# A decoder block's query weights asked for earlier, its expert numbers put first, its head squares summed on another engine

## The chip, the cores and the metric

The kernel runs on one core of one Trainium2 chip. A core has a matrix engine (TensorE, PE in the profile, with its weight loads as PEld), a vector engine (VectorE, DVE), a scalar engine (ScalarE, ACT), a general engine (GpSimd, POOL), a queue engine that issues most transfers (SyncE, SP) and 16 DMA engines that carry them out. Every engine works through its own instructions in order and waits for semaphores of the others. The metric is the device time of one execution in microseconds (us).

## What is computed

One decoder layer over 512 tokens of width 1024, in float32. Three attention branches (a forgetting attention, a windowed one and one over 256 memory tokens) are mixed with sigmoid gates, projected and added to x. Then each token looks up experts: its query, 8 heads of 2 x 128, is scored against 2 x 128 keys, the best 16 of each half are paired, the best 16 pairs of each head name 128 of the 16384 experts, and

```
experts = e1 * N_KEYS + e2
gates = softmax(sv)
a[e] = dot(h, u[experts[e]])
out = sum_e gelu(a[e]) * gates[e] * v[experts[e]]
```

Queries and keys of the attention branches are normalised by head first: each head's 64 (or 128) values are squared and summed, and the head is scaled by one over the root of the mean.

## The kernel before

The 512 tokens are four blocks of 128. Block 0 goes through the mixers alone (`mixers(0, ...)`), and then blocks 1 to 3 go through them together (`mixers(1, ...)`, `BIG` = 3 blocks). While the three are mixed, block 0's expert search and its expert rows run beside them: `beside()` is a generator, and `pump()`, called at every load of weights and by every head of the attentions, lets it go on by some steps. After the mixers the three blocks are searched, and then all experts are computed densely for blocks 2 and 3 (the long stage from about 720 us on), while blocks 0 and 1 go on gathering single expert rows.

The order in which each engine gets its instructions up to the dense stage is laid out ahead of time by a planner. It simulates the kernel on a timeline of its own, with priorities that follow the program's order. What `pump()` issues after the search is put 400 steps later in priority, so that it fills gaps. A dependency that only fixes an order (`add_manual_dep` with `NoSync`) keeps one instruction behind another in that planning. From the dense stage on the order of PE, DVE and POOL is the one written.

Block 0's search (`search` with one block) takes 16 tiles of query weights of 512 KB each, two per head. `fetch` asks for a tile on SP's queue when its product is issued. The tiles turn over in four slots: three lie in the buffer that will hold the three blocks' merged branches (`mg1`), one (`raw`) in memory that the first mixers' weights occupied. PE multiplies (line 766), ACT copies the query out (767), PE scores it against the keys (774), ACT copies the scores (777), and DVE picks the best 16 of each half and of the pairs (lines 731 to 735).

After that, in `beside()`: `weigh` makes the softmax of the found values (lines 801 to 813, on DVE with one exponential on ACT), and `numbers_of` turns the found positions into expert numbers (`choose`, lines 828 to 858, then 868 and 869) and makes block 0's normalised row `own` (line 872). Then `step` asks POOL for each expert's row (line 908), and DVE multiplies it with `own` and sums (line 929) or adds it into the output (lines 936, 939, 942). 184 such rows are issued beside the mixers.

In the mixers, `heads` computes one group of queries or keys: products (lines 152 to 154, three for each pair of split operands), then in `use`, for each block, a copy out of PSUM on ACT (348), the square of the product on ACT (350) and the sum by head on DVE (351). `rsqrt_mean` (209 and 210) makes the factors, and ACT scales each head by its factor (363). Buffers for queries (`qT`) and for the branch output (`ohi`, `olo`) have one slot each.

Of the kernel before, what the change touches and what calls it, by code (L numbers as in the profile page):

```python
# [8 lines left out]
F32 = mybir.dt.float32  # L9
# [4 lines left out]
AF = mybir.ActivationFunctionType  # L14
OP = mybir.AluOpType
AX = mybir.AxisListType

S, D, NB, KC = 512, 1024, 4, 8
NMEM = 256
EPS = 1e-6  # L20
TOPK = 16
# [38 lines left out]
def tile_block(ctx: ExitStack, tc: tile.TileContext, t: dict, out: bass.AP):  # L60
# [98 lines left out]
    def wide(tag, nb, dt=F32):  # L159

        slot = big.tile([128, (1 if tag == "mg0" else BIG) * D], dt, tag=tag, name=tag)
        return slot[:, :nb * D]

    def by_token(x):
        return x.rearrange("p (b d) -> p b d", d=D)
# [175 lines left out]
    def heads(lhs, src, nb, nh, hd, pad=0, n=None, also=None, fetch=None, cast=None):  # L341

        z = pp.tile([128, BIG, 4 * 66], F32, tag="qn", name="qn")
        z = z[:, :nb, :nh * (hd + pad)].rearrange("p b (h d) -> p b h d", h=nh)
        ss = small_f(BIG * 4, "hss")[:, :nb * nh]

        def use(b, ps):
            A.copy(z[:, b, :, :hd], ps[:, :nh * hd].rearrange("p (h d) -> p h d", h=nh))
            sq = pp.tile([128, 256], F32, tag="sq", name="sq")[:, :nh * hd]
            A.square(sq, ps[:, :nh * hd])  # L350
            V.reduce_sum(ss[:, b * nh:b * nh + nh], sq.rearrange("p (h d) -> p h d", h=nh), axis=AX.X)
            if also:
                also(b, ps)

        gemm_nat(lhs, src, n or nh * hd, nb, use, fetch=fetch, cast=cast)
        r = rsqrt_mean(ss, nb * nh, hd)
        for b in range(nb):
            if nb < BIG:
                V.tensor_mul(z[:, b, :, :hd], z[:, b, :, :hd],
                             r[:, b * nh:b * nh + nh, None].to_broadcast([128, nh, hd]))  # L360
                continue
            for h in range(nh):
                A.activation(z[:, b, h, :hd], z[:, b, h, :hd], AF.Copy, scale=r[:, b * nh + h:b * nh + h + 1])
        return z
# [429 lines left out]
        yield from top_pairs(PH - 1)  # L794


    def weigh(pool, f, g):

        nb = len(GROUPS[g])
        ex = pool.tile([128, nb, PH, TOPK], F32, name="ex")  # L800
        V.tensor_sub(ex, f.best, f.best[:, :, :, 0:1].to_broadcast([128, nb, PH, TOPK]))
        for b in range(nb):
            bf = ex[:, b].rearrange("p h s -> p (h s)")
            ins = A.activation(bf, bf, AF.Exp, scale=rstd[:, GROUPS[g][b]:GROUPS[g][b] + 1])
            if b:
                tc.keep_in_program_order(ins)
        yield 0.4
        den = small.tile([128, BIG * PH], F32, tag="gden", name="gden", bufs=1)[:, :nb * PH]
        dv = den.rearrange("p (b h) -> p b h", b=nb)
        V.reduce_sum(dv, ex, axis=AX.X)  # L810
        V.reciprocal(den, den)
        for b in range(nb):
            V.tensor_mul(gates_of[g][:, b].rearrange("p s h -> p h s"), ex[:, b],
                         dv[:, b, :, None].to_broadcast([128, PH, TOPK]))
        yield 1.0
# [42 lines left out]
            V.tensor_add(dst[i], hv[:, 0], hv[:, 1])  # L858
            yield 1.4

    def numbers_of(pool, f, lb, b, iota_k):

        g2r = pool.tile([128, D], F32, name="g2r")
        row = t["g2_row"]
        nc.sync.dma_start(g2r, bass.AP(tensor=row.tensor, offset=row.offset, ap=[[0, 128], [1, D]]))
        e = [pool.tile([128, NJ], F32, tag=f"e{i}", name=f"e{i}") for i in range(2)]
        yield from choose(pool, f, lb, iota_k, e)
        V.scalar_tensor_tensor(e[0], e[0], float(NK), e[1], op0=OP.mult, op1=OP.add)
        V.tensor_copy(eidx[b], e[0])
        if b == 0:  # L870
            h2n[0] = h2n[1] = ep.tile([128, D], F32, tag="own", name="own")
        V.scalar_tensor_tensor(h2n[b], x1[b], rstd[:, b:b + 1], g2r, op0=OP.mult, op1=OP.mult)
        yield 1.3


# [74 lines left out]
    def beside():  # L950
# [3 lines left out]
        with tc.tile_pool(name="qa", bufs=2, side="right") as qq:  # L954
            h2T = chunks(qq.tile([128, KC, 128], F32, name="aT", bufs=1))
            behind.append(turn([x1[0]], g2, h2T, None).ins.name)
            V.tensor_copy(rstd[:, 0:1], factors(sums, 1))
            yield 0.0
            lent, turns = by_token(wide("mg1", BIG)), [0]

            def fetch(src, n):
                i = turns[0] % (BIG + 1)
                turns[0] += 1
                raw = lent[:, i] if i < BIG else qq.tile([128, D], F32, tag="raw", name="raw", bufs=1)
                fill(raw, src, n)
                return raw

            yield from search(qq, h2T, f, 1, fetch)
        pace[0] = "choose"
        share[0] = 0.0  # L970
        with tc.tile_pool(name="ca", bufs=1, side="right") as pool:
            iota_k = iota_of(pool)
            yield from weigh(pool, f, 0)
            yield from numbers_of(pool, f, 0, 0, iota_k)
        kept.close()
        pace[0], share[0] = "rows", 0.0
        credit[0] += 20.0
# [445 lines left out]
```

## Time and profile before

| | |
|---|---|
| three runs | 1552.81, 1552.13 and 1544.93 us, median 1552.13 |
| profiled execution | 1548.8 us, its span from first to last instruction 1547.0 us |
| mean granted TensorE clock | 0.99 |
| PE, DVE, ACT, POOL busy | 97%, 92%, 53% and 50% of the span |
| DMA | 533.48 MB, mean 345 GB/s |

The profile is one execution, recorded by the hardware. A row of a timeline gives the start and the duration in us, the engine, the line of the kernel, the operation, what it writes and reads, its shape, and in brackets how long the engine had been idle before it and what released it. A row of waits gives who waited for whom, then the total in us, the number of times and the longest. Busy time of PE is no measure of its efficiency, since products overlap.

### The profile page before, as it was taken

The numbers are of one execution on the slowest core, as the hardware profiler recorded it, in microseconds if no ns is written. First come the engines' busy times: TensorE is split into PE (matmuls) and PEld (weight loads), VectorE is DVE, ScalarE is ACT, GpSimd is POOL, SyncE is SP. The second block draws the span as 40 slices with busy tenths as digits, with TensorE's granted clock in tenths as the row PEclk, the third lists the DMA queues.
The fourth block names the chain that finished last, engine by engine and source line by source line (L and its number), as shares of the span: only waits on it lengthen the run. The fifth ranks groups of instructions, "written<-read, shape, count | busy, mean of one in ns | idle before, by whom it ended". The sixth has DMA issues, their size and how long they took to land.

```text
span 1547.0 us, 27092 instructions
## 1 busy us (share of the span) xinstructions
PE 1498.3 (97%) x9411; PEld 1360.5 (88%) x9411; DVE 1419.4 (92%) x2673; ACT 812.4 (53%) x1806; POOL 778.1 (50%) x642
## 2 busy tenths in 40 slices
PE   8999999999999989999999999999999999999998
PEld 7999899997897989999888887788888888888887
DVE  6689488989999999999999999899999999999998
ACT  7778346646345533352225899545444544544543
POOL 1101016767667456877445666545554544555451
PEclk9999999999998999999999999999999999999999
DMA  8688657998999898986998999999999999999995
GB/s 325 207 289 300 246 174 280 338 362 302 360 367 325 293 356 317 352 310 232 327 365 329 393 395 384 373 397 398 401 410 403 408 410 404 411 410 410 410 410 209
DMA packets 180125, 533.48 MB, mean 345 GB/s; under 512 B 17660, under 2 KB 48148, under 8 KB 179988
## 3 DMA queue, kind: packets, MB, share of 16 engines
q0 software_dynamic: 73728, 268.47, 45.9%
q1 hardware_dynamic: 96180, 227.54, 40.1%
q10 hardware_dynamic: 10080, 35.75, 5.8%
q8 instruction: 74, 1.21, 0.3%
q14 instruction: 63, 0.52, 0.1%
HBM read 516.99 MB, written 14.69 MB: 344 GB/s over the span
## 4 chain that ended last, share of the span: by engine, by line
PE 52%; issue 14%; DMA 11%; POOL 9%; DVE 9%; ACT 4%; POOLq 0%; DVEq 0%; SPq 0%; ACTq 0%
PE mm L153 9%; PE mm L152 9%; PE mm L154 9%; POOL row L908 9%; PE mm L1078 5%; DMA row<-in_peer_v_dram,eidx 4%; DMA row<-in_peer_u_dram,eidx 3%; PE sc L1078 3%; DVE wlo L138 2%; DMA gd<-st 2%; PE mm L766 2%; DVE o L1144 2%; DVE scr L929 1%; PE tp L384 1%; PE sc L506 1%
## 5 line engine op out<-in xcount | busy, mean ns | idle before, releaser
L908 POOL DMA_INDIRECT row<-in_peer_v_dram,eidx x256 | 322.2, 1258 | 298.3 <-DVE two L942 175.5
L908 POOL DMA_INDIRECT row<-in_peer_u_dram,eidx x256 | 315.4, 1232 | 219.8 <-DVE scr L929 115.8
L138 DVE TENSOR_TENSOR wlo<-raw,whi 128x1024 fp32r<-128x1024 f32 (+1 forms) x228 | 277.2, 1220 | 21.7 <-ACT whi L123 17.5
L942 DVE SCALAR_TENSOR_TENSOR two<-row,acts,two 128x1024 f32<-128x1024 f32 x197 | 252.6, 1282 | 5.3 <-DMA row<-in_peer_v_dram,eidx 3.1
L123 ACT CAST whi<-raw 128x1024 fp32r<-128x1024 f32 x146 | 152.2, 1050 | 119.2 <-PE mm L153 75.4
L929 DVE SCALAR_TENSOR_TENSOR scr<-row,own 128x1024 bf16<-128x1024 f32 x128 | 156.2, 1220 | 7.1 <-DMA row<-in_peer_u_dram,eidx 6.4
L929 DVE SCALAR_TENSOR_TENSOR scr<-row,two 128x1024 bf16<-128x1024 f32 x115 | 139.5, 1213 | 3.8 <-DMA row<-in_peer_u_dram,eidx 2.9
L210 POOL TENSOR_TENSOR rsy<-rsv,mhalf 128x4 f32<-128x4 f32 (+5 forms) x25 | 37.8, 1515 | 177.2 <-DVE rsv L209 176.3
L1212 ACT CAST ah<-ga 128x256 fp32r<-128x256 f32 x116 | 47.1, 407 | 150.2 <-PE tp L153 125.0
L152 PE MATMUL mm<-hhi,whi 128*128 128x384 f32 x320 | 110.8, 346 | 1.8 <-ACT hhi L244 1.4
L153 PE MATMUL mm<-hlo,whi 128*128 128x384 f32 x320 | 110.7, 346 | 0.0
L154 PE MATMUL mm<-hhi,wlo 128*128 128x384 f32 x320 | 109.9, 343 | 0.0
L152 PE MATMUL mm<-whi,hhi 128*128 128x256 f32 (+1 forms) x360 | 103.6, 290 | 2.7 <-ACT hhi L681 1.9
L1214 ACT CAST whi<-raw 128x1024 fp32r<-128x1024 f32 x96 | 100.3, 1047 | 9.5 <-DMA raw<-in_peer_v_dram 4.6
L153 PE MATMUL mm<-wlo,hhi 128*128 128x256 f32 (+1 forms) x360 | 102.7, 286 | 1.3 <-DVE wlo L138 1.3
L153 PE MATMUL sc<-wlo,ah 128*128 128x512 f32 x256 | 101.2, 395 | 2.5 <-DVE wlo L138 2.5
L152 PE MATMUL sc<-whi,ah 128*128 128x512 f32 x256 | 100.8, 394 | 1.3 <-ACT whi L1214 1.2
L154 PE MATMUL mm<-whi,hlo 128*128 128x256 f32 (+1 forms) x360 | 102.0, 285 | 0.0
L154 PE MATMUL sc<-whi,al 128*128 128x512 f32 x256 | 101.2, 395 | 0.0
L153 PE MATMUL tp<-wlo,ah 128*128 128x512 f32 x256 | 101.1, 395 | 0.0
L152 PE MATMUL tp<-whi,ah 128*128 128x512 f32 x256 | 101.0, 395 | 0.0
L154 PE MATMUL tp<-whi,al 128*128 128x512 f32 x256 | 100.6, 393 | 0.0
(332 smaller groups left out, 4478.2 us busy)
## 6 DMA issues: line engine op xcount, KB each, us to landing
raw<-in_peer_v_dram SPq DMA_DIRECT2D x96, 512.0 KB
hhi<-in_uT_dram ACTq DMA_DIRECT2D x68, 512.0 KB
raw<-in_w_tr_dram SPq DMA_DIRECT2D x48, 512.0 KB
raw<-in_w_nat_dram SPq DMA_DIRECT2D x40, 512.0 KB
last<-in_peer_v_dram SPq DMA_DIRECT2D x32, 512.0 KB
hhi<-in_uT_dram SPq DMA_DIRECT2D x26, 512.0 KB
raw<-in_w_o_dram SPq DMA_DIRECT2D x24, 512.0 KB
gd<-st SPq DMA_DIRECT2D x24, 512.0 KB
```

The source lines that it names most:

```text
L123: ins = (cast or A.copy)(hi[:, :n * w], raw[:, :n * w])
L138: V.tensor_sub(lo, raw, hi.bitcast(F32))
L152: PE.matmul(ps, lh, rh, start=first, stop=False)
L153: PE.matmul(ps, lh, rl, start=False, stop=False)
L154: PE.matmul(ps, ll, rh, start=False, stop=last)
L210: G.tensor_tensor(y, v, mhalf[:, :n], op=OP.pow)
L908: ins = G.indirect_dma_start(out=r, out_offset=None, in_=t["peer_" + tab], in_offset=bass.IndirectOffsetOnAxis(ap=eidx[b][:, j:j + 1], axi ...
L929: V.scalar_tensor_tensor(scr, r, 1.0, two[0] if b else h2n[b], op0=OP.mult, op1=OP.mult, accum_out=acts[b][:, c]))
L942: V.scalar_tensor_tensor(two[0], r, acts[b][:, c], two[0], op0=OP.mult, op1=OP.add))
L1078: PE.matmul(ps[:, :TD], w[:, dc], h2f[dc], start=dc == 0, stop=dc == KC - 1)
L1212: A.copy(ah, a)
L1214: A.copy(hi, raw)
```

## The change

It has three parts.

1. `fetch` has seven slots in place of four: the same three of `mg1`, the one called `raw`, and one each in the buffers `qT`, `ohi` and `olo`. At the first product it asks for seven tiles, and at each later one for the next tile, up to 16.
2. `numbers_of` goes before `weigh`. An order-only dependency (`follow`) puts the weighing's first instruction and the row `own` behind the copy of the expert numbers.
3. In `heads`, where three blocks are worked on together, ACT squares each head by itself out of the copy `z` and sums it with the same instruction (`accum_out`). The square of the whole group and DVE's sum by head are left out there. Block 0 and the memory tokens keep the earlier way.

```diff
@@ heads / use
-            A.square(sq, ps[:, :nh * hd])
-            V.reduce_sum(ss[:, b * nh:b * nh + nh], sq.rearrange("p (h d) -> p h d", h=nh), axis=AX.X)
+            if nb == BIG:
+                for h in range(nh):
+                    A.activation(sq[:, h * hd:(h + 1) * hd], z[:, b, h, :hd], AF.Square,
+                                 accum_out=ss[:, b * nh + h:b * nh + h + 1])
+            else:
+                A.square(sq, ps[:, :nh * hd])
+                V.reduce_sum(ss[:, b * nh:b * nh + nh], sq.rearrange("p (h d) -> p h d", h=nh), axis=AX.X)
@@ weigh
+    def follow(ins, after):
+        if after:
+            tc.add_manual_dep(ins.ins, after[-1], mybir.DependencyInfo(
+                mybir.DependencyClass.NoSync, mybir.DependencyReason.DATA), reason="behind the numbers")
+
-    def weigh(pool, f, g):
+    def weigh(pool, f, g, after=()):
...
-        V.tensor_sub(ex, f.best, f.best[:, :, :, 0:1].to_broadcast([128, nb, PH, TOPK]))
+        follow(V.tensor_sub(ex, f.best, f.best[:, :, :, 0:1].to_broadcast([128, nb, PH, TOPK])), after)
@@ numbers_of
-    def numbers_of(pool, f, lb, b, iota_k):
+    def numbers_of(pool, f, lb, b, iota_k, done=None):
...
-        V.tensor_copy(eidx[b], e[0])
+        ins = V.tensor_copy(eidx[b], e[0])
+        if done is not None:
+            done.append(ins.ins.name)
...
-        V.scalar_tensor_tensor(h2n[b], x1[b], rstd[:, b:b + 1], g2r, op0=OP.mult, op1=OP.mult)
+        follow(V.scalar_tensor_tensor(h2n[b], x1[b], rstd[:, b:b + 1], g2r, op0=OP.mult, op1=OP.mult), done)
@@ beside
-            lent, turns = by_token(wide("mg1", BIG)), [0]
+            lent = by_token(wide("mg1", BIG))
+            slots = [lent[:, i] for i in range(BIG)] + [qq.tile([128, D], F32, tag="raw", name="raw", bufs=1)]
+            slots += [pp.tile([128, 4, BIG * 128], F32, tag=tag, name="raw", bufs=1).rearrange("p a b -> p (a b)")[:, :D]
+                      for tag in ("qT", "ohi", "olo")]
+            asked, taken = [0], [0]
 
             def fetch(src, n):
-                i = turns[0] % (BIG + 1)
-                turns[0] += 1
-                raw = lent[:, i] if i < BIG else qq.tile([128, D], F32, tag="raw", name="raw", bufs=1)
-                fill(raw, src, n)
-                return raw
+                i = taken[0]
+                taken[0] += 1
+                while asked[0] < min(i + len(slots), 2 * PH):
+                    fill(slots[asked[0] % len(slots)], t["w_pq"][asked[0]], n)
+                    asked[0] += 1
+                return slots[i % len(slots)]
...
-            yield from weigh(pool, f, 0)
-            yield from numbers_of(pool, f, 0, 0, iota_k)
+            numbered = []
+            yield from numbers_of(pool, f, 0, 0, iota_k, numbered)
+            yield from weigh(pool, f, 0, numbered)
```

## The prediction

> **What bounds the kernel now.** I read the page's totals first, then the busy time by stages, then the waits and the order of time in the stages that the change touches.
>
> ```profile
> span 1547.0 us, 27092 instructions
> PE 1498.3 (97%) x9411; PEld 1360.5 (88%) x9411; DVE 1419.4 (92%) x2673; ACT 812.4 (53%) x1806; POOL 778.1 (50%) x642
> ```
>
> TensorE is idle for only 1547.0 - 1498.3 = 48.7 us, and VectorE for 128. ScalarE is free half of the time. By stages (columns: stretch, its length, busy us of PE, PEld, DVE, ACT, POOL, clock, DMA share, GB/s):
>
> ```profile
> 177.00:212.40 35.40, 32.83 (x291) 32.28 (x289) 24.07 (x150) 10.90 (x32) 5.40 (x25) 1.00 0.79 276
> 212.40:244.00 31.60, 31.60 (x271) 31.60 (x270) 29.68 (x112) 20.21 (x60) 7.42 (x11) 1.00 0.31 102
> 244.00:480.00 236.00, 231.68 (x1603) 211.80 (x1602) 214.73 (x404) 128.75 (x326) 168.45 (x126) 1.00 0.95 346
> 480.00:500.00 20.00, 16.36 (x75) 13.90 (x75) 18.98 (x37) 9.57 (x24) 16.29 (x12) 0.74 0.95 333
> 560.00:630.00 70.00, 62.45 (x426) 59.85 (x425) 68.59 (x82) 26.39 (x52) 41.02 (x29) 0.93 0.90 317
> 630.00:720.00 90.00, 88.97 (x541) 87.13 (x540) 87.15 (x492) 36.95 (x63) 70.98 (x70) 1.00 0.82 304
> 1000.00:1500.00 500.00, 496.63 (x2908) 437.58 (x2907) 489.13 (x570) 243.96 (x355) 252.85 (x186) 1.00 1.02 406
> ```
>
> Block 0's search lies in the first stretch, its expert numbers in the second, the three blocks' mixers with the gathered rows from 244 to about 630, their search after that. From 1000 to 1500 PE lacks 3.4 us of 500: what is left there is work, so that a shift before it should pass through to the end. What can be won before 630 is PE's idle time, 2.6 + 0 + 4.3 + 3.6 + 7.6 = 18.1 us in the five stretches shown, and time at a lowered clock: (1 - 0.74) x 20 + (1 - 0.93) x 70 = 10.1 us. In 560 to 630 DVE is full (68.59 of 70) and PE waits for it:
>
> ```profile
> PE mm L152 <- DVE g L618: 2.2, 2, 1.4
> PE mm L152 <- ACT hhi L681: 1.9, 1, 1.9
> ```
>
> Both are products of DVE or come right behind them, and the gathered rows, 1.2 us each, are what else is in DVE's queue.
>
> The lowered clock follows waits of PE. The wait that opens the stretch at 480 is this one:
>
> ```profile
> 482.67 0.44 PE L384 MATMUL tp<-cst,p 128*128 128x128 f32 x2 [2.12 <-ACT p L547]
> ```
>
> [...]
>
> **Part 1, seven weight tiles.** Four slots of 512 KB turn over in block 0's search. PE stops for them:
>
> ```profile
> 188.71 3.84 PE L766 MATMUL mm<-aT,mg 128*128 128x128 f32 x32 [1.31 <-DMA mg<-in_w_pq_dram]
> ...
> 193.62 2.05 PE L766 MATMUL mm<-aT,raw 128*128 128x128 f32 x16 [1.07 <-DMA raw<-in_w_pq_dram]
> ```
>
> ```profile
> 157.52 0.80 SPq L117 DMA_DIRECT2D mg<-in_w_pq_dram  x2
> ...
> 184.84 0.33 SPq L117 DMA_DIRECT2D raw<-in_w_pq_dram  x1
> ```
>
> The tile asked for at 184.84 is the one that PE takes at 193.62: 8.8 us. A tile with its share of scores costs PE 32.83 / 16 = 2.05 us. Four slots give 4 x 2.05 = 8.2 us of lead, less than 8.8; seven give 14.4. So these waits, 1.31 + 1.07 = 2.4 us of the stretch's 2.6 idle, go. The first seven asks are now ahead of the search: three more transfers, 1.5 MB, on SP's queue, near the ones that already go out at 157.52, 20 us before the search. At the 276 GB/s of the first stretch they take 5.7 us, inside that time. If they stood behind the fourth tile, whose buffer comes free only shortly before the search, they would still land within 14 us, and tile 4 isn't read before 177 + 4 x 2.05 = 185.2. Bounds of this part: 0 (they come late or push the mixers' weights back) to -2.4; I take -2.4, as 14.4 is far over 8.8. The borrowed buffers (query, and the two halves of the branch output) are next written by the mixers' own code after 244, when the search is over: no new wait.
>
> **Part 2, numbers first.** Between search and rows DVE does this (first and last of the weighing's four instructions, the normalised block, the numbers, the first row):
>
> ```profile
> 220.70 0.29 DVE L801 TENSOR_TENSOR ex<-best 128x128 f32<-128x128 f32 x1
> ...
> 225.50 0.41 DVE L813 TENSOR_TENSOR gate<-ex,gden 128x128 f32<-128x128 f32 x1
> ...
> 225.82 1.28 DVE L872 SCALAR_TENSOR_TENSOR own<-mg,rstd,g2r 128x1024 f32<-128x1024 f32 x1
> ...
> 241.11 0.23 DVE L869 CAST eidx<-e 128x128 int32<-128x128 f32 x1
> ...
> 249.53 1.23 DVE L929 SCALAR_TENSOR_TENSOR scr<-row,own 128x1024 bf16<-128x1024 f32 x1 [5.06 <-DMA row<-in_peer_u_dram,eidx]
> ```
>
> ```profile
> 242.34 1.58 POOL L908 DMA_INDIRECT row<-in_peer_u_dram,eidx  x1 [5.18 <-ACT sq L350]
> ```
>
> Moved behind the numbers: the weighing, 4 x about 0.25 = 1.0 us, and the block's 1.2 us (1.28 less overlap). Neither is late there. The block is read by the first row at 249.53, 7.2 us after POOL asks for it; the weighing's result is wanted only when all 128 rows of u are through. With part 1's 2.4 us and some five reductions, about 1.5 us, gone from this stretch (part 3), the numbers come 2.4 + 1.0 + 1.2 + 1.5 = 6.1 us sooner, near 235, and the first gather near 236. POOL sits idle before 242.34, so nothing is pushed back by it but the small powers on the same queue, by at most one gather, 1.58 us. If all of this is only slack, its worth is 0; if DVE bounds without a break until 720, it is 6.1.
>
> **Part 3, squares on ScalarE.** Removed from DVE and from ACT in the three blocks (210 to 490; durations are minimum, median and maximum in ns):
>
> ```profile
> L351 DVE TENSOR_REDUCE hss<-sq x27: 270/412/421, 216.1 to 480.4; 128x4 f32<-128x256 f32 x18, 128x2 f32<-128x256 f32 x6, 128x2 f32<-128x128 f32 x3
> ```
>
> ```profile
> L350 ACT ACTIVATE sq<-mm x27: 283/390/415, 215.8 to 479.7; 128x256 f32<-128x256 f32 x24, 128x128 f32<-128x128 f32 x3
> ```
>
> ```profile
> 259.27 0.41 DVE L351 TENSOR_REDUCE hss<-sq 128x4 f32<-128x256 f32 x1
> 259.60 1.21 DVE L929 SCALAR_TENSOR_TENSOR scr<-row,own 128x1024 bf16<-128x1024 f32 x1
> ```
>
> From start to next start a reduction takes 0.33 us: 24 x 0.33 + 3 x 0.2 = 8.5 us of DVE. ScalarE gets 90 squares with a sum instead of 27: four for each of 18 (72) and two for each of 9 (18), 12 of them 128 wide (the memory heads), 78 of them 64 wide. No row shows a 64-wide square. The nearest show the steps:
>
> ```profile
> 479.70 0.39 ACT L350 ACTIVATE sq<-mm 128x256 f32<-128x256 f32 x1
> 479.97 0.59 ACT L378 ACTIVATE qT<-tg,gcol 128x384 f32<-128x384 f32 x1
> ```
>
> ```profile
> 482.05 0.47 ACT L547 ACTIVATE p<-sc,nm 128x256 f32<-128x256 f32 x1 [0.56 <-DVE nm L543]
> 482.43 0.19 ACT L547 ACTIVATION_READ_ACCUMULATOR p<-sc,nm 128x1 f32 x1
> 482.52 0.47 ACT L547 ACTIVATE p<-sc,nm 128x256 f32<-128x256 f32 x1
> ```
>
> A 256-wide square holds ACT 0.27 us and the read of a sum 0.09 us. From 390 ns at 256 and 283 ns at 128, a 64-wide one lasts 283 - 54 = 229 ns and holds ACT about 0.11 us. So a 64-wide square with its sum costs between 0.11 + 0.09 = 0.20 and 0.47 us (the 256-wide exponent with its sum); I take 0.25, nearer the low end because the shape is a quarter of that, and 0.30 for 128. Sum 78 x 0.25 + 12 x 0.30 = 23.1 us, less the 24 x 0.27 + 3 x 0.17 = 7.0 us removed: +16 us of ACT (bounds 78 x 0.20 + 12 x 0.26 - 7.0 = +12 and 90 x 0.47 - 7.0 = +35). ACT has 236 - 128.75 = 107 us free between 244 and 480, which hides it on the mean. It is not hidden where ACT is dense:
>
> ```profile
> 260.00:270.00 10.00, 10.00 (x81) 9.41 (x81) 9.92 (x22) 8.45 (x20) 6.04 (x7) 1.00 1.01 388
> 270.00:280.00 10.00, 10.00 (x79) 8.92 (x78) 9.24 (x20) 8.27 (x26) 8.59 (x6) 1.00 0.83 286
> ```
>
> There 16.7 of 20 us are taken, and some six squares of a block fall into it, each growing by 4 x 0.25 - 0.27 = 0.73 us: 4.4 us into 3.3 us of room, 1 us over. Behind them in ACT's order stand the casts of the next weights, which PE waits for. I cost this at +1 us (bounds 0 and, at 0.47 a square, 6 x 1.61 - 3.3 = +6.4). In return the sums no longer stand behind DVE's rows, and the bank of PSUM is free after the copy.
>
> [...]
>
> **The sum.** DVE is relieved by 8.5 us of reductions, and rows begin 6.1 us sooner; 1.5 of it is in both, so 13.1 us less can stand in front of PE by 560. Between 244 and 480 DVE has 21 us idle, so some of that only becomes more idle time; from 560 to 720 it is full. I let half arrive: -6.6, less than the 7.6 us idle and 4.9 us of clock that stand in 560 to 630 (bounds 0 and -13.1). The chain at 482 loses a reduction, 0.33, and about one row of 1.2 us that its sums stand behind: -1.5. So -2.4 - 6.6 - 1.5 + 1 = -9.5 us. The profiled execution took 1548.8 us (1.8 beyond its span), and the median of the three runs, 1552.1, lies 3.3 above that. So 1539.3 on the one and 1542.6 on the other; I say 1541, which is -9.5 from their middle, 1550.5, and the rivals go from there. A change under 0.5% (7.8 us) can't be told from none here.
>
> **Rivals.** (a) Only the search's waits go, -2.4: 1548. The freed DVE time becomes idle, since PE and DVE alternate as the bound. For it: DVE's 21 us idle before 480. Against: DVE full from 560. (b) The stalls shrink together with the clock that follows them. The 18.1 us idle and 10.1 us of clock are all there is to win, 28.2; two thirds of it are -19: 1532. (c) Slower: ACT becomes the bound where queries and keys are made, since the squares stand before the casts. It decides from about 0.47 us a square: 6.4 us over, with a stretch like that at 480 behind it, 5.2 us of clock, less the search's 2.4, DVE's relief lost meanwhile: +9, 1560. For it: ACT at 8.3 to 8.5 of 10; against: its free 107 us, and that ACT's order is laid out anew. (d) The extra asks don't come early, because they stand on SP's queue behind the fourth tile until the search begins, when the mixers' weights are asked for too: the search's 2.4 stays, and half as much of the rows' lead with it, -9.5 + 3.6 = -6: 1545.
>
> **How the numbers follow.** Forecast 45% (own range 1534 to 1547), (a) 16%, (b) 18%, (c) 15%, (d) 6%. The 8-in-10 range runs from 1526, for a (b) that takes nearly all, to 1557, most of the way to (c). Faster by over 0.5% is below 1542.7: (b) and two thirds of the forecast, 0.48. Slower: (c), and 2% for a mishap in the order that no case names, 0.17. Within: the rest, 0.35.
>
> **What would show it.** Right: no PE wait for query weights in block 0's search; the first gather near 236; 90 squares at about 0.25 us each and no reduction by head in the three blocks; the three blocks' search starts 8 to 10 us sooner. Wrong: the first gather near 242, PE waits for casts between 250 and 290 with a lowered clock, or the same start of the three blocks' search.

## The result and the profile after

The changed kernel is slower: a median of 1570.5 us (1566.8 to 1571.9), against 1552.1 us (1544.9 to 1554.9) for the kernel before, timed beside it. The ratio is 1.012, with a 95% interval of 1.0102 to 1.0138: 18 us more, where 9.5 us less were forecast.

The totals of the page of the changed kernel:

```profile
span 1567.0 us, 27212 instructions
PE 1511.5 (96%) x9411; PEld 1369.7 (87%) x9411; DVE 1409.2 (90%) x2646; ACT 827.6 (53%) x1959; POOL 778.3 (50%) x642
```

VectorE has 10.2 us less work and ScalarE 15.2 us more, as costed (8.5 of reductions; +16). TensorE's idle time went from 48.7 to 55.5 us, and its busy time rose by 13 us with the same 9411 instructions. In part that is the clock: added up from stretches of 1 us, TensorE ran 47.8 us at half clock, against 30.7 before, and half of the difference is 8.5 us. The other 4.7 us of it are not put down to anything here. By stages (the same stretches as before, and 380 to 400; columns: stretch, length, busy us of PE, PEld, DVE, ACT, POOL, clock, DMA share, GB/s):

```profile
177.00:212.40 35.40, 35.40 (x310) 35.09 (x309) 23.15 (x143) 11.40 (x33) 5.39 (x25) 1.00 0.70 255
212.40:244.00 31.60, 28.85 (x230) 28.34 (x229) 25.55 (x105) 18.39 (x82) 8.46 (x10) 0.95 0.28 101
244.00:480.00 236.00, 230.07 (x1489) 206.29 (x1488) 202.91 (x370) 131.84 (x406) 163.62 (x123) 0.96 0.91 333
380.00:400.00 20.00, 18.50 (x70) 13.67 (x71) 18.23 (x38) 9.34 (x30) 16.45 (x13) 0.51 0.91 329
480.00:500.00 20.00, 20.00 (x156) 17.93 (x155) 18.02 (x37) 14.29 (x50) 14.84 (x12) 1.00 0.93 334
630.00:720.00 90.00, 84.07 (x524) 82.69 (x525) 79.20 (x388) 39.87 (x71) 69.34 (x60) 0.98 0.82 293
```

The search runs without a wait (35.40 of 35.40), as forecast. The loss begins right behind it: TensorE is idle for 2.8 us between 212.4 and 244, where it had no idle time before. The lowered clock that stood at 480 is gone from there: that work now comes some 20 us later, and the clock is halved beside it for 6.8 us, from 503 us on. A longer stretch stands at 380: 0.51 over 20 us, 10 us of clock by 0.49 x 20. VectorE, relieved, is idle more: 33 us between 244 and 480 instead of 21. The first query of the three blocks' search is copied 22 us later than before, and from the dense stage on the distance is 21 us and no longer changes.

The timelines of VectorE and GpSimd round the expert numbers show the rows:

```profile
241.59 0.22 DVE L879 CAST eidx<-e 128x128 int32<-128x128 f32 x1
...
251.30 0.40 DVE L823 TENSOR_TENSOR gate<-ex,gden 128x128 f32<-128x128 f32 x1
```

```profile
252.70 1.15 POOL L920 DMA_INDIRECT row<-in_peer_u_dram,eidx  x1 [11.95 <-ACT sq L352]
```

The numbers are there at 241.8, half a microsecond later than before and not near 235 (31.6 us behind the search's last product with query weights, where it was 28.7), and the first gather comes at 252.70, not near 236. It comes 1 us behind the last instruction of the weighing. The reason is in the memory: the row buffers are opened over the memory that the search's findings and the weighing's scratch tile `ex` held, so that the first gather has to wait for the last reader of both (the run with the scratch moved, below, shows it for `ex`). Before, that reader stood ahead of the numbers and had long been done.

### The profile page after: what moved, and what is told of

The parts are those of the page before. It is cut to its first block, busy times and chain, and to the rows that moved or that the text cites. A ratio compares the mean times of both kernels' runs of the same rounds, so it can differ in the third digit from the quotient of the medians.

```text
span 1567.0 us, 27212 instructions
## 1 busy us (share of the span) xinstructions
PE 1511.5 (96%) x9411; PEld 1369.7 (87%) x9411; DVE 1409.2 (90%) x2646; ACT 827.6 (53%) x1959; POOL 778.3 (50%) x642
## 4 chain that ended last, share of the span: by engine, by line
PE 54%; issue 13%; DMA 10%; DVE 9%; POOL 9%; ACT 5%; POOLq 0%; DVEq 0%; SPq 0%; ACTq 0%
PE mm L152 8%; PE mm L154 8%; PE mm L153 8%; POOL row L920 7%; PE mm L1096 7%; DMA row<-in_peer_v_dram,eidx 4%; DMA row<-in_peer_u_dram,eidx 4%; PE sc L1096 3%; PE sc L1177 2%; DVE wlo L138 2%; PE mm L771 2%; PE sc L153 1%; PE sc L154 1%; PE acc L518 1%; PE tp L153 1%
## 5 line engine op out<-in xcount | busy, mean ns | idle before, releaser
L954 DVE SCALAR_TENSOR_TENSOR two<-row,acts,two 128x1024 f32<-128x1024 f32 x197 | 252.7, 1283 | 5.2 <-DMA row<-in_peer_v_dram,eidx 3.0
```

What stands on the lines that cost most here:

```text
L954: V.scalar_tensor_tensor(two[0], r, acts[b][:, c], two[0], op0=OP.mult, op1=OP.add))
```

## The experiments

**The theories.** T1: the late rows cost the 18 us. T2: the squares do, since they stand in ScalarE's order ahead of scales and casts (the prediction's rival c). T3: the seven slots do. T4: none of the parts by itself, but the order of all instructions, which the planner lays out anew once any of them changes. How far it does so can be read off the two programs: even with the slots alone, which touch only transfers of the search, TensorE's instructions stand in another order from 389 us on, 176 us behind the search's end.

Medians and ratios to the kernel before, each timed beside it (what each kernel is stands below):

| kernel | us | ratio, 95% interval |
|---|---|---|
| changed kernel | 1570.5 | 1.0120 (1.0102 to 1.0138) |
| slots alone | 1559.0 | 1.0053 (1.0036 to 1.0069) |
| numbers first alone | 1566.7 | 1.0101 (1.0084 to 1.0118) |
| squares alone | 1568.9 | 1.0091 (1.0055 to 1.0126) |
| slots and squares | 1554.1 | 1.0022 (1.0001 to 1.0042) |
| all three, scratch moved | 1572.1 | 1.0133 (1.0107 to 1.0159) |
| **order of before held:** slots | 1549.8 | 0.9986 (0.9973 to 1.0000) |
| held: squares | 1552.7 | 1.0005 (0.9990 to 1.0021) |
| held: slots and squares | 1549.8 | 0.9984 (0.9967 to 1.0001) |
| held: all three | 1553.0 | 1.0018 (1.0004 to 1.0031) |
| held: all three, scratch moved | 1551.0 | 0.9991 (0.9973 to 1.0009) |
| held: slots, later squares only | 1547.6 | 0.9978 (0.9965 to 0.9991) |
| held: that and numbers first, scratch moved | 1551.4 | 1.0002 (0.9987 to 1.0017) |
| held: slots and numbers first, scratch moved | 1552.7 | 1.0005 (0.9991 to 1.0020) |
| held: slots, later squares, six instructions moved | 1553.5 | 1.0012 (0.9995 to 1.0029) |
| kernel before in the changed kernel's order (PE, POOL) | 1580.5 | 1.0187 (1.0166 to 1.0208) |
| all three, held up to 300 us only | 1559.9 | 1.0075 (1.0049 to 1.0101) |
| all three, held from 300 us only | 1554.9 | 1.0026 (1.0012 to 1.0039) |
| all three, held for PE and POOL only | 1568.2 | 1.0112 (1.0090 to 1.0134) |

A trace is one execution. At 152 us, where all these kernels have done the same work, the profiled ones already lie up to 5 us apart (the mean clock up to 177 us is 0.97 with the squares alone and 1.00 with the numbers first alone, by an estimate 0.03 x 177 = 5 us). So a distance in a trace counts from the search on, and a kernel's price is read from the ratios.

### The parts alone

The slots alone are the change's hunk in `beside` (`fetch`):

```diff
-            lent, turns = by_token(wide("mg1", BIG)), [0]
+            lent = by_token(wide("mg1", BIG))
+            slots = [lent[:, i] for i in range(BIG)] + [qq.tile([128, D], F32, tag="raw", name="raw", bufs=1)]
...
+                while asked[0] < min(i + len(slots), 2 * PH):
```

> The kernel before with the seven slots alone; weighing first and the reductions on VectorE as before. Theories for the +18 us of the whole change. T1 (the rows): the weighing behind the numbers holds the memory that the row buffers lie over, and the rows start some 10 us late; this part is then innocent: 1549 to 1552, -2.4 to 0 (TensorE's waits for query weights in block 0's search gone, first gather near 240). T2 (the squares): ScalarE's order with 90 squares stalls casts and scales; this part again -2.4 to 0. T3 (the seven slots): the three more asks on SP's queue push the mixers' weights back and the +2.3 us before the search and what follows come from here: 1555 to 1570. T4 (a new order laid out by the planner, whatever the part): each part alone moves the time by several us up or down, with lowered-clock stretches at other places.

Measured: +0.53%. The stalls of the search are gone, and until 388 us the kernel is 0.5 us ahead of the one before. Then TensorE takes another instruction next. Its timeline in the kernel before, and with the slots alone:

```profile
388.86 0.43 PE L554 MATMUL acc<-sv,pT 128*128 128x64 f32 x2 [1.01 <-ACT pT L386]
```

```profile
389.60 0.44 PE L152 MATMUL mm<-ohi,whi 128*128 128x384 f32 x1 [2.25 <-DVE mg L616]
```

A product with a VectorE result (`mg`) now stands ahead of the window's P times V; it waits 2.25 us where 1.01 us were waited before. By the three blocks' search the kernel is 11.5 us behind. T1 and T2, which called this part innocent, don't explain it; T3 and T4 do.

The numbers first alone (the hunks in `weigh`, `numbers_of` and the order of the two calls):

```diff
-            yield from weigh(pool, f, 0)
-            yield from numbers_of(pool, f, 0, 0, iota_k)
+            numbered = []
+            yield from numbers_of(pool, f, 0, 0, iota_k, numbered)
+            yield from weigh(pool, f, 0, numbered)
```

> The kernel before with the order of numbers and weighing changed alone. T1: the first gather comes behind the weighing's last instruction, later than the 242.3 us of the kernel before by 5 to 12 us although the numbers are ready 1 to 2 us earlier; time 1558 to 1568, most of the +18. T2: the first gather no later than 242, time 1548 to 1552. T4: any time, with the loss in stretches of lowered clock rather than in the rows.

Measured: +1.01%, and the first gather at 250.3 although the numbers were copied at 239.7. T1's sign is there; but the attentions' exponents ran up to 8.6 us ahead of the kernel before until 340 us, and were 5.9 us behind at 382.

The squares alone (the hunk in `heads`):

```diff
+            if nb == BIG:
+                for h in range(nh):
+                    A.activation(sq[:, h * hd:(h + 1) * hd], z[:, b, h, :hd], AF.Square,
+                                 accum_out=ss[:, b * nh + h:b * nh + h + 1])
```

> The kernel before with the squares on ScalarE alone. T2: TensorE waits for ScalarE's scales and casts between 225 and 300 us and a stretch of lowered clock follows; 1557 to 1570. T1: 1545 to 1552, VectorE 8 to 10 us less busy, first gather near 241. T4: any time, not explained by either wait.

Measured: +0.91%. Three of its four executions lay at 1568.5 to 1569.5 us and one at 1559.1: a difference of 10 us in one and the same program. T2's size, so far.

The changed kernel with the weighing back in front:

```diff
-            numbered = []
-            yield from numbers_of(pool, f, 0, 0, iota_k, numbered)
-            yield from weigh(pool, f, 0, numbered)
+            yield from weigh(pool, f, 0)
+            yield from numbers_of(pool, f, 0, 0, iota_k)
```

> The changed kernel with the weighing put back ahead of the numbers (slots and squares kept). T1: the first gather near 240, time 1545 to 1553, 17 us or more below the changed kernel. T2: still 1560 or more, with the waits for ScalarE at 230 to 236 and at 380. T3: still 1560 or more, with TensorE's waits before and after the search. T4: between, e.g. 1550 to 1565, with lowered clock somewhere else.

Measured: +0.22%. Two parts that cost 0.53% and 0.91% each cost 0.22% together. T2 and T3 can't be right as prices of a part: they would have to add. Taking part 2 out of the whole wins about 1%, and putting it in alone costs 1%, which fits T1.

### The late rows, taken away

The changed kernel with one edit: the weighing computes in the gates' own memory, which the row buffers don't touch.

```diff
-        ex = pool.tile([128, nb, PH, TOPK], F32, name="ex")
+        ex = gates_of[g].rearrange("p b s h -> p b h s")
...
-            bf = ex[:, b].rearrange("p h s -> p (h s)")
+            bf = gates_of[g][:, b].rearrange("p s h -> p (h s)")
```

> The changed kernel, all three parts, in the planner's order, with one edit: the weighing computes in the gates' own memory and no longer in a tile that the row buffers lie over. T1 (the rows are late by the weighing): the first gather comes within 2.5 us of the copy of the numbers, near 243 instead of 252.7, and the time falls by 10 us or more, to 1550 to 1560. T4 alone: the first gather near 243 too, the time not below 1562. If the rows wait for something else, the first gather stays near 250.

GpSimd's timeline in that kernel:

```profile
244.40 1.15 POOL L920 DMA_INDIRECT row<-in_peer_u_dram,eidx  x1 [4.89 <-ACT qn L368]
```

The first gather comes 8.3 us sooner than in the changed kernel, as T1 said, and the time did not fall: +1.33%. T1 has the mechanism right and the price wrong, as far as a kernel can show it that the planner has laid out anew once more; the held pair below has the order the same.

### The order held

To tell T4 from the others, the order in which the kernel before issues its instructions was written into the kernel and kept with order-only dependencies, for TensorE, ScalarE and GpSimd from the start and for VectorE from about the end of block 0's search. These are no waits: they decide only what stands behind what in the layout.

```diff
+ORDER = {
+    "PE": (
...
+def _pin(tc):
...
+            if prev is not None:
+                tc.add_manual_dep(mine[at], mine[prev].name, mybir.DependencyInfo(
+                    mybir.DependencyClass.NoSync, mybir.DependencyReason.DATA), reason="order of before")
+            prev = at
...
         tile_block(tc, aps, res)
+        _pin(tc)
```

With the slots alone:

> The seven slots alone, with the instructions of TensorE, ScalarE, VectorE and GpSimd held in the order that they have in the kernel before (only SyncE's asks stand elsewhere). T4 (the planner's new order costs the time): the search's 3 us stay won to the end, 1546 to 1549, 9 to 13 us below the same slots in the planner's order (1559). T3 (the slots themselves cost it): 1555 to 1561 again.

Measured: 0.9986 of the kernel before, -2.2 us (interval -4.2 to 0), against +0.53% in the planner's order. With the squares alone, each square's place taken by its two or four squares with sums:

> The squares on ScalarE alone, with the four engines held in the order of the kernel before: each square's place is taken by its two or four squares with sums, the reductions by head are left out of VectorE's order, all else stands as it stood. T4: 1542 to 1550, below the kernel before, against 1569 in the planner's order. T2 (the squares hold up scales and casts in ScalarE's order): 1555 or more, with TensorE waiting for ScalarE between 225 and 300 and at 380 to 400 as in the changed kernel.

Measured: 1.0005, no change, against +0.91%. That is not T2's 1555, but T4's gain isn't there either. With both:

> Slots and squares together, with the four engines held in the order of the kernel before. T4: 1538 to 1547, what the two parts gain where nothing is laid out anew (-3 of the search and a part of VectorE's 8.5 us), less than in the planner's order (1554). T2 or T3: 1553 or more.

Measured: 0.9984, or 1549.8 us, between the two forecasts. T2 and T3 fall as the cause: the same work with the same extra squares in the old order costs nothing. T4 has the loss right; the gain that it expected of the parts isn't there. The weighing moved as well (its five instructions and the row `own` left to the planner, behind the numbers):

> The whole change, with TensorE, ScalarE, VectorE and GpSimd held in the order of the kernel before; only the weighing's exponent on ScalarE and its four instructions and the normalised block on VectorE stand behind the numbers. T4 (the new order costs the +18 us): 1546 to 1554, 17 us or more below the changed kernel, although the first gather still waits for the weighing. T1 (the late rows cost): 1558 or more. Both: 1553 to 1560.

Measured: 1.0018, against 1.0120 for the same three parts in the planner's order: 1.02%, 16 of the 18 us, are the order. Its clock between 300 and 480 us is full again, and the stretch of 0.51 is gone:

```profile
300.00:480.00 180.00, 177.07 (x1179) 161.41 (x1178) 165.01 (x306) 95.15 (x265) 125.60 (x96) 1.00 0.95 348
```

The same with the scratch moved:

> The same held order, and the weighing in the gates' own memory, so that the first gather need not wait for it. T1: 6 us or more below the whole change in the held order. T4: within 3 us of it, 1546 to 1552, although the first gather is some 8 us sooner.

Measured: 0.9991, below the one with the late rows by 2 us in the medians and 4 us in the ratios; the intervals overlap. GpSimd's timeline in the one with the late rows, and with the scratch moved:

```profile
248.15 2.17 POOL L920 DMA_INDIRECT row<-in_peer_u_dram,eidx  x1 [9.30 <-ACT whi L123]
```

```profile
245.95 1.91 POOL L920 DMA_INDIRECT row<-in_peer_u_dram,eidx  x1 [5.68 <-ACT qn L348]
```

The copies of the numbers begin at 241.79 and 243.20, so that the first gather comes 6.4 and 2.8 us behind them. In this order the weighing ends sooner than in the changed kernel (11.1 us there), and moving its scratch wins 3.6 us for the rows and not the 8 that were expected. That is worth 2 to 4 us. Rows that come 10 us late were not tried in the old order.

And the other way round, the kernel before with none of the parts, TensorE and GpSimd held in the order of the changed kernel:

> The kernel before with none of the three parts, but with the instructions of TensorE and GpSimd held in the order that the planner gave the changed kernel (ScalarE, VectorE and SyncE follow it). T4: the order alone brings most of the loss, 1560 to 1572, with the three blocks' search 10 us or more later than in the kernel before. If the parts themselves cost the time: 1549 to 1555.

Measured: +1.87%, 29 us, more than expected. ScalarE and VectorE are laid out anew here, so this is a mixed order and not the changed kernel's own; what it shows is that an order alone can cost this much with none of the parts. Its longest waits of TensorE between 212 and 660 us:

```profile
PE mm L152 <- DVE g L618: 5.3, 4, 1.9
PE mm L152 <- ACT v L491: 4.3, 1, 4.3
PE sc L535 <- ACT p L547: 4.1, 1, 4.1
```

None of the three is among the kernel before's longest there, except the first with 2.2 us. The order was laid for other durations, and TensorE stands in front of products whose inputs aren't ready.

### Where in the order

The whole change, held up to about 300 us of the trace, and then laid out anew; and the reverse, the planner's own order up to there and the order of before behind it. The edit is the same `ORDER`, cut at the 30th gather and its neighbours on the other engines.

```diff
-    "PE": places 0 to 8168
+    "PE": places 0 to 1919
...
-    "PE": places 0 to 8168
+    "PE": places 1920 to 8168
```

> The whole change, the four engines held in the order of the kernel before only up to about 300 us of its trace; behind that the planner lays the work out anew. The changed kernel lost 13 us between the search's end and 300 us and 9 us from there to the three blocks' search. If the two stretches add: 1560 to 1565, 9 us or so above the order held throughout (1553). If all of it follows from the late start: 1550 to 1556. If it follows from what the planner does later: 1566 or more.

> The whole change, in the planner's own order up to about 300 us and from there in the order of the kernel before. If the two stretches add: 1562 to 1568, some 12 us above the order held throughout. If the rest follows from the late start, 1568 or more; if the loss lies in the later order alone, 1550 to 1556.

Measured: +0.75% and +0.26%, where the order held throughout gave +0.18%. Most of it lies behind 300 us, and the two don't add up to the changed kernel's 1.20%: 0.57 and 0.08 above the held order. In the second kernel the attentions' exponents were 12 us behind the kernel before at 287 us, 5.5 us at 308, and 4.4 to 5.5 us from there on: the early order does more of what comes later, and in the old order behind it half of the delay is got back. What the planner lays out behind 300 us in the first kernel isn't the changed kernel's own order either, so these two say where most of it lies and not what every stretch costs.

Holding TensorE and GpSimd only:

```diff
-    "Activation": (
...
-    "DVE": (
...
```

> The whole change with TensorE and GpSimd alone held in the order of the kernel before; ScalarE and VectorE as the planner then lays them. If TensorE's order is what costs: within 3 us of the four engines held (1553). If it is how ScalarE and VectorE stand: 1560 or more.

Measured: +1.12%, nearly all of the loss, with TensorE in the order of before. So it isn't TensorE's order by itself. What costs lies in how ScalarE and VectorE stand beside it; those two were not held alone.

### The dense stretch, and the squares behind it

In the held order the way from the search's end to the exponents near 270 us is 4.4 us longer with all squares on ScalarE than in the kernel before, and 0.8 us longer with the slots alone. ScalarE's timeline at the keys' heads, with the slots alone and with slots and squares, both held:

```profile
237.47 0.35 ACT L348 COPY qn<-mm 128x256 f32<-128x256 f32 x1
237.73 0.38 ACT L350 ACTIVATE sq<-mm 128x256 f32<-128x256 f32 x1
238.00 1.04 ACT L123 CAST whi<-raw 128x1024 fp32r<-128x1024 f32 x1
```

```profile
240.49 0.35 ACT L348 COPY qn<-mm 128x256 f32<-128x256 f32 x1
240.87 0.26 ACT L352 ACTIVATE sq<-qn 128x64 f32<-128x64 f32 x1
...
241.84 1.03 ACT L123 CAST whi<-raw 128x1024 fp32r<-128x1024 f32 x1
```

From the copy to the cast of the next weights it was 0.53 us and is 1.35: each square group holds ScalarE 0.8 us longer, as costed (0.73), and here the casts and the scaled heads stand behind it. One kernel keeps the squares on ScalarE for the window's and the memory's queries alone:

```diff
-            if nb == BIG:
+            if nb == BIG and not pad and nh * hd == 256:
```

> Slots, and the squares on ScalarE for the window's and the memory's queries alone (12 of 27; from about 280 us on), with the four engines held in the order of the kernel before. In that order all 27 squares lengthened the stretch from the search's end to the first exponent near 270 by 4.5 us (TensorE waits for the scaled keys behind them). If that is rival (c) on a small scale, this kernel does not show it: -2 us up to 300, and 1545 to 1549 at the end. If the 4.5 us come from elsewhere, they stay: 1549 to 1552.

Measured: 0.9978, the fastest of all kernels here and the only one whose interval lies below 1, though it overlaps that of the slots alone. But on that way it still loses 2.5 us, by a TensorE wait of 2.6 us for a weight remainder in place of one of 1.3; and all three parts with the scratch moved, which have all the squares, lose only 1.4 us there. So the early squares have a price in that stretch, but which one hangs on what stands beside them.

With the numbers first and the scratch moved added to it, and the same without any square on ScalarE (both diffs as above):

> Everything that did no harm, together: the slots, the numbers first with the weighing in the gates' own memory, and the squares on ScalarE for the window's and the memory's queries, with the four engines held in the order of the kernel before. If the numbers' lead of some 2 us is worth anything in that order: 1544 to 1547, below the same kernel with the weighing first (1547.6). If VectorE has slack there: 1547 to 1549.

> The same without any square on ScalarE: slots and numbers first, order held. The slots alone gave 1549.8 in that order. If the later squares are worth 2 us: 1547.5 to 1550, 2 us above the run with them. If they are worth nothing there: equal to it within 1 us.

Measured: 1.0002 and 1.0005, 4 and 3 us above the same kernels with the weighing first (0.9978 and 0.9986). So part 2 doesn't help even with its memory mended. Against VectorE's queue the numbers didn't get any sooner: their copy is done 28.8 us behind the search's last product with query weights when the weighing stands behind them, and 28.7 with it in front. VectorE is busy 25.3 us of that way instead of 26.8 and waits longer for ScalarE (for its squares 1.30 us instead of 0.69), so what was taken out of its queue became idle time. TensorE's wait in the first of the two:

```profile
PE tg L382 <- ACT qn L368: 2.9, 1, 2.9
```

The queries' scale factors come from GpSimd, whose power for them stands behind six gathers in its order. The gathers began 4.2 us behind the numbers instead of 1.2, since the row `own` and the weighing's first instruction stand between, and so the power came later too. In the profiled executions of this pair the whole distance, 5.4 us, stands at the search's end already, and none comes with the numbers; in the second pair 3.6 of 4.7 us come behind them. So that part 2 wins nothing is shown, and its price is not. The later squares make 0.5 us here (1.0002 against 1.0005) and 1.2 us above (0.9978 against 0.9986), both inside the intervals.

### Six instructions by hand

In the held kernel with the later squares TensorE waits 1.9 us at 481.7, with a mean clock of 0.74 over the 20 us round it, the place that the prediction had quoted of before. ScalarE's last window exponents and VectorE's step ahead of them were moved forward, a cast and a weight remainder back:

```diff
 VectorE:  max(last scores)
+          max with sink
           wlo
           row
-          max with sink
-          wlo (next)
           rsv
+          wlo (next)
 ScalarE:  whi, pT
+          p, p
           copy qn, squares, qT
-          whi (next), p, p, pT, es
+          pT, whi (next), es
```

> The slots and the later squares in the order held (1547.6), with nothing but six instructions moved by hand near 478 us: on VectorE the maximum with the sink ahead of a weight remainder, and the mean's first step ahead of another; on ScalarE the last window exponents ahead of a copy and its squares, and two casts behind. TensorE's wait of 1.9 us at 481.7, behind which the clock is at half for 10 us, should fall below 1 us. If the clock follows that wait: 1540 to 1544. If the stretch of half clock comes whatever the waits there: 1545 to 1548.

Measured: 1.0012, 5 us worse than without the edit. TensorE's timeline in that kernel, and VectorE's and ScalarE's:

```profile
491.64 1.65 PE L382 MATMUL tg<-cst,qn 128*128 128x128 f32 x3 [2.85 <-ACT qn L368]
```

```profile
488.62 1.23 DVE L138 TENSOR_TENSOR wlo<-raw,whi 128x1024 fp32r<-128x1024 f32 x1 [2.71 <-ACT whi L123]
```

```profile
491.09 0.20 ACT L550 ACTIVATE es<-es 128x2 f32<-128x2 f32 x1 [2.51 <-DVE es L549]
```

The wait at the exponents is gone, and a longer one stands 5 us further on in the work: the cast put back holds VectorE's remainder for 2.71 us, behind the remainder and a row stands the small difference `es`, behind its exponential on ScalarE stand the scaled queries, and for these TensorE waits 2.85 us. The clock over the 20 us is 0.74 again:

```profile
480.00:500.00 20.00, 14.16 (x70) 10.12 (x69) 16.00 (x33) 11.01 (x33) 13.99 (x12) 0.74 0.90 314
```

The eight products ahead of this wait, at 487.69, take 1.10 us (as many take 1.00 at 478.77 and 1.97 at 483.81 in the kernel without the edit), and the three behind it take 1.65. With 0.74 over the 20 us, 10.4 us of them are at half clock, and from 500 us on the mean is 1.00 again, so the clock falls no later than about 1 us into this wait, and behind two others of 1.13 and 0.67 us. So the mean is the same with the wait at the exponents and without it. Nor do the rows explain the 5 us: of the 6.9 us between the two profiled executions 5.0 are there at 475 us, ahead of the edited place. What they do show is a size: with one cast in another place a wait of 2.9 us comes up.

## Why the prediction was wrong

**Part 1, right.** No wait for query weights is left. -2.4 was predicted, and -2.2 measured in the order held (interval -4.2 to 0). The asks come early: six of them are out before 175 us in the changed kernel, so rival (d) is not it.

**Part 2, wrong in "Neither is late there".** The weighing's result is wanted late, but its scratch memory is wanted at once, by the row buffers. The first gather moved from 242.3 to 252.7. The step looked for who reads the moved instructions' results and left out who reuses their memory. Mended, it still brings nothing: the numbers, forecast 6.1 us sooner, came 0.5 us later in the changed kernel and no sooner behind the search in the held order. What was taken out of VectorE's queue, 1.5 us of work in the held order, became idle time, and "by at most one gather" for the powers on GpSimd's queue was wrong too: in the old order six gathers stand ahead of the queries' power, and when they come late it does.

**Part 3, right in its durations and wrong in its worth.** A 64-wide square was costed at 0.25 us with its sum. The groups of ScalarE's instructions in the changed kernel have (busy us, mean ns; some records are missing):

```profile
L352 ACT ACTIVATE sq<-qn 128x64 f32<-128x64 f32 x78 | 19.1, 252 | 0.2
L352 ACT ACTIVATION_READ_ACCUMULATOR sq<-qn 128x1 f32 x88 | 17.1, 194 | 0.0
```

Square and read overlap: the next square starts 0.24 us after the one before. ScalarE's +16 was +15.2. But the place where ScalarE is dense was costed at +1 us, and the stretch up to 270 grew by 1.4 to 4.4 us in the held order, and all 27 squares are worth nothing by themselves (1.0005).

**The sum's middle term, wrong.** "I let half arrive: -6.6". In the order held, where it can be seen by itself, VectorE's relief by the later squares brought at most about 1 us (0.9978 against 0.9986 and 1.0002 against 1.0005), by all 27 0.3 us (0.9984 against 0.9986), and the rows didn't begin sooner by part 2. VectorE's share of the time before 560 turned into idle time, as rival (a) had it. The chain at 482, -1.5, kept its wait, 1.9 us instead of 2.1, and its mean clock of 0.74 over 20 us. The smaller waits behind it in the kernel before, 0.68 us ahead of 484.44 and 0.67 us ahead of 488.38, stand behind the fall of the clock, which comes at 483.66 and lasts 10.24 us there.

**What the sum left out.** Even with these terms mended it would have said about -2, and the kernel became 18 us slower. Every term took a duration from a row of before and moved it as if all else stayed where it was. The front of this document says that the order is laid out ahead by a planner; the prediction used that once, as a point *against* rival (c) ("ACT's order is laid out anew"), allowed 2% for "a mishap in the order", and put it at nothing in the sum. Its price is 16 of the 18 us. In five pairs of the same work the planner's new order cost 0.67% (slots), 0.86% (squares), 0.38% (both), 1.02% (all three) and 1.42% (all three, scratch moved) over the old one. Every one of them is a loss. The kernel before with TensorE and GpSimd in the changed kernel's order lost 1.87%.

Rival (c), at 15%, had the right sign and a part of the right place: the lowered clock did come, at 380 and not at 250 to 290. But the squares are not its cause: in the old order the same squares leave the time as it was.

What stays open is why the planner's new layouts fit the chip worse than the one of before: which of its durations is off was not tried. Nor is there one wait to which the 16 us could be put down; between the profiled executions of the two kernels 8.5 of 20 us are the clock.

## What to carry to other kernels

Where a planner lays out the order, a change has two prices: what its instructions cost where they stand, and what the new order of all the others costs. The second is read by holding the old order round the change, and here it was more than five times the first (1.02% against 0.18%). Before moving an instruction, look not only for who needs its result but also for who is given its memory next. VectorE, 90 to 92% busy here, wasn't relieved by taking work out of its queue where what came next in that queue waited for another engine: 1.5 us less of it beside the numbers became idle time, and the time did not fall (1.0002 against 0.9978).

## What the runs showed of the hardware

**The clock stood at half for 3.4 to 20.5 us at a time, and the longest of these stretches began behind a wait of 0.90 us.** The changed kernel's stretch of 0.51, in stretches of 2 us (columns as above):

```profile
378.00:380.00 2.00, 1.10 (x9) 0.88 (x8) 2.00 (x5) 0.78 (x2) 1.36 (x2) 1.00 1.03 393
380.00:382.00 2.00, 2.00 (x7) 1.11 (x8) 2.00 (x5) 0.58 (x1) 2.00 (x1) 0.64 0.96 375
382.00:384.00 2.00, 1.18 (x5) 0.48 (x3) 2.00 (x6) 1.65 (x7) 1.50 (x3) 0.50 0.72 293
...
400.00:402.00 2.00, 2.00 (x11) 1.90 (x11) 1.97 (x4) 1.07 (x2) 1.70 (x2) 0.74 0.87 311
402.00:404.00 2.00, 2.00 (x14) 1.47 (x12) 1.97 (x5) 1.14 (x2) 1.39 (x3) 1.00 0.86 283
```

It begins at 380.55 and ends at 401.03, 20.48 us at 0.50. TensorE's waits round its beginning:

```profile
379.87 1.44 PE L511 MATMUL sc<-kT,qT 66*128 66x512 f32 x2 [0.90 <-issue]
383.26 0.47 PE L382 MATMUL tg<-cst,qn 128*128 128x128 f32 x1 [0.56 <-ACT qn L368]
384.22 0.47 PE L382 MATMUL tg<-cst,qn 128*128 128x128 f32 x1 [0.48 <-ACT qn L368]
386.12 1.97 PE L518 MATMUL acc<-v,pT 128*128 128x64 f32 x8 [0.36 <-ACT pT L391]
```

Only the first, 0.90 us until 379.87, stands ahead of the fall; the other three come when the clock is halved already. With all three parts in the held order these stand in the same stretch of work:

```profile
381.63 1.10 PE L518 MATMUL acc<-v,pT 128*128 128x64 f32 x8 [0.68 <-ACT pT L391]
388.97 0.44 PE L410 MATMUL tp<-cst,o 128*128 128x128 f32 x2 [0.30 <-DVE o L406]
390.29 0.27 PE L540 MATMUL sc<-distb,slope 128*128 128x256 bf16 x1 [0.18 <-ACT p L552]
392.98 0.45 PE L153 MATMUL mm<-olo,whi 128*128 128x384 f32 x1 [0.77 <-DVE olo L148]
396.44 0.43 PE L559 MATMUL acc<-sv,pT 128*128 128x64 f32 x2 [1.01 <-ACT pT L391]
```

The longest is 1.01 us and the sum 2.9, and the clock between 300 and 480 stays at 1.00, as quoted above. So neither the longest wait nor the sum decides it.

In the profiled executions of the kernel before and of the changed one every stretch of half clock up to 1500 us lasted a whole number of times 3.41 us: 6.8, 10.2, 3.4, 6.8 and 3.4 us before, and 6.8, 3.4, 3.4, 20.5, 6.8, 3.4 and 3.4 in the changed kernel. Their beginnings, too, were whole numbers of times 3.41 us apart: in the changed kernel 380.55 and 503.43 lie 36 times that from each other, and 1001.78 comes 146 times behind the second; before, 12.62 and 483.66 lie 138 times apart. Both executions have a stretch of 6.8 us in the opening work (from 12.62 and 11.91 us on; the mean clock up to 177 us is 0.98 and 0.97), while that of the numbers first alone has a mean of 1.00 up to there. What brings a fall about isn't shown. In the changed kernel TensorE is busy for 2.51 of the 3.41 us ahead of the fall at 380.55, and 39 times 3.41 us earlier only for 1.82, without a fall behind it:

```profile
377.14:380.55 3.41, 2.51 (x13) 1.51 (x13) 3.41 (x8) 1.04 (x3) 2.73 (x3) 1.00 0.99 382
247.43:250.84 3.41, 1.82 (x14) 1.62 (x15) 2.20 (x4) 3.40 (x6) 0.00 (x0) 1.00 0.37 117
```

The kernel with the squares alone came out 10 us apart (1568.5 to 1569.5 and 1559.1). By an estimate the clock makes some 5 to 6 us of it: its mean is 0.985 to 0.986 in the three and 0.989 in the other, and 0.003 to 0.004 of 1569 us is that much.

**The same small power on GpSimd took 4.45 us in one kernel and 1.40 us in another.** It works on 128x6 values, in the changed kernel and with all three parts in the held order:

```profile
226.11 4.45 POOL L210 TENSOR_TENSOR rsy<-rsv,mhalf 128x6 f32<-128x6 f32 x1 [7.50 <-DVE rsv L209]
```

```profile
224.42 1.40 POOL L210 TENSOR_TENSOR rsy<-rsv,mhalf 128x6 f32<-128x6 f32 x1 [4.34 <-DVE xf L433]
```

ScalarE's scales waited 3.7 us for the first and 1.4 us for the second. VectorE worked beside both (4.38 of the 4.45 us in the changed kernel). What makes the difference isn't shown: no run here changed one instruction beside the power alone.
